# Retention's gated result: from a DRAM round trip to parts formed out of the transposes' PSUM banks, with the head's pieces moved by a step

## Chip, cores and metric

One NeuronCore of a Trainium2 chip runs the whole program. The metric is device time in microseconds (us) of one execution: the median of three timed runs, with lowest and highest. Beside them stands one execution under the hardware profiler, from which all rows of the trace come.

## The reference

A decoder trunk of two layers on 512 tokens of width 2048, in float32. Layer 0 is multi-scale retention, layer 1 latent attention; the change lies in layer 0 and at its output projection.

```python
proj = h @ w_in
q, k, v, g = jnp.split(proj, [RET_QK, 2 * RET_QK, 2 * RET_QK + RET_WIDTH], axis=-1)
q = rope(q.reshape(B, S, RET_HEADS, RET_DK), pos)              # 8 heads of 256
k = rope(k.reshape(B, S, RET_HEADS, RET_DK), pos) * (RET_DK ** -0.5)
v = v.reshape(B, S, RET_HEADS, RET_DV)                         # 8 heads of 512
y = chunkwise_retention(q, k, v)
mu = jnp.mean(y, axis=-1, keepdims=True)
var = jnp.mean(jnp.square(y - mu), axis=-1, keepdims=True)
y = (y - mu) * lax.rsqrt(var + EPS)
y = (y.reshape(B, S, RET_WIDTH) * gn_g.astype(jnp.float32)).astype(h.dtype)
return (jax.nn.silu(g) * y) @ w_out                            # 4096 -> 2048
```

Around it stand RMSNorm with a modulated shift and scale (`ada_w`, computed from the conditioning vector), a modulated gate and a residual add.

## The kernel before

**Exact parts.** Every product of two float32 matrices runs as three TensorE (PE) matmuls on two parts: `hi` is the value rounded to the matmul's format and `lo` the rest, and hi\*hi, hi\*lo and lo\*hi are summed in PSUM (`mm3`, L157). The helper `split` (L132) makes them: ScalarE (ACT) copies the source into `hi` (L133) and VectorE (DVE) subtracts (L134).

**Steps.** The middle of the program is a list of steps. One step holds the weights of one unit (load by SP, `split` on ACT and DVE), its matmuls, what follows them (copies out of PSUM), and `beside`: extra loads, forms and matmuls of other work. For step i the driver (L1290 on) issues, in this order: weight loads for up to three steps ahead, the step's extra loads, the split of the weights of step i+1, the extra forms, the step's matmuls, its extra matmuls, the additions of a "modulation row" that was loaded at the end of the step before, the load of the next row, and the copies that follow. `behind` keeps each engine's queue in that order; a small amount of reordering is left to the scheduler. Weights of a step are 128 x 2 x 512; raw, high and low tiles have three buffers each. A modulation row (L820, L829) is a 512 KB load and one DVE operation, later summed on PE by matmuls with one output column (`sum_modulation`, L842), in steps marked `banks_free`.

**Blocks.** I call sixteen steps a block. Block p is the query/key projection of heads 6 and 7. Blocks n = 0 to 3 are the output projection, contraction rows of heads 2n and 2n+1: in each block four rounds r (512 output columns) of four units u, 24 matmuls of 512 columns a step. A unit u reads the input parts `o1_in[n, u]` (two row blocks of 128 features); units 0 and 1 come from the even head, 2 and 3 from the odd one. Running sums stay in four `acc` banks in a round; at its end ACT keeps them in SBUF (L1060) and from n=1 on seeds the next round from there (L1057).

**A head beside the steps.** `retention(h)` (L887) returns a list of pieces, one for each step. Heads 0 and 1 run beside block p, 2 and 3 beside block 0, and so on; the even head's piece k stands in step k, the odd head's in step k+4. Before the change there are 13 pieces:

| piece | load | form (ACT, DVE) | matmuls |
|---|---|---|---|
| 0 | `load_qk(0)` | | |
| 1, 2 | `load_qk(1)` in 2 | rotary, query halves | |
| 4, 5 | `load_decay` in 5 | rotary, key halves | |
| 7 | | | `scores`, into four `aux` banks |
| 8 | `load_v` | `decay_scores` (L932) | |
| 9 | `load_gates` | `split_v` | `values`, into four `aux` banks |
| 10 | | `group_norm` (L959 to L971) | |
| 11 | | `gate` (L977) | `transposes` (L984), into four `aux` banks |
| 12 | | `store` (L992, L994) and DMA on POOL's queue (L996) | |

Queries, keys, values and gates wait in DRAM from the projection. There are four `aux` banks, so each use has to wait until the banks of the one before are read. For head 0, silu of the gate multiplies after the transposes (L994), for the others before (L977).

**The way to the projection.** `store` multiplies the transposed result by the norm's gain and POOL writes it to `y2_d`, four blocks of 128 rows a head. `o1_input` (L1080) loads two such blocks at a time on SP's queue into one tile with a single buffer (L1087) and splits it with L133 and L134. These loads and splits stand in the last two steps of a block and the first three of the next, beside the weights of those steps. In the profile the tiles are called `y` or `y_d`, `o_in`, `o_h` and `o_l`, and the projection's weights `o_r`, `o_whi`, `o_wlo`.

**Shared buffers that the change touches.** `tmp`: six tiles of 128 x 512. `big`: sixteen tiles for parts; they hold the layer's input until block p has read it, then rotary queries and keys, values, and the projection's input parts. `yn`: four tiles, for raw values as well as normalised rows, and for copies of head 7's queries and keys on their way to DRAM.

## Time and profile before

| | us |
|---|---|
| median of three runs (lowest, highest) | 2272.65 (2268.16, 2273.11) |
| the profiled execution | 2269.27 |
| its span, first to last instruction | 2267.5 |
| TensorE busy in the span | 2195.1 |
| VectorE busy | 1522.6 |
| ScalarE busy | 992.5 |
| mean granted TensorE clock | 0.99 |

Times in the trace count from the span's start. Block p runs from about 943 to 1060, the blocks 0 to 3 from 1060 to about 1510. A row of a group reads: line, engine, operation, output<-inputs, sizes and count, then busy time in us, mean ns of one, and idle time of the engine before them with what ended it. A row of waits reads: who waited for whom, total us, times, the longest. Neighbouring instructions of one engine overlap a little at their ends in these records, so that a row of several can be shorter than their sum.

### The profile page before, as it was taken

The page shows a single profiled execution, that of the slowest core. Times are in us where ns is not written, and L with a number is a line of the kernel's source. Part 1 is how long each engine was busy: PE and PEld are TensorE (multiplying, and loading weights), DVE is VectorE, ACT ScalarE, POOL GpSimd, SP SyncE. Part 2 cuts the span into 40 slices and gives each one's busy share as a digit, 9 for nine tenths or more (in the row PEclk, how much of TensorE's full clock was granted, in tenths as well). Part 3 has the DMA queues.
Part 4 walks back from the last instruction along what each step waited for, and adds up shares of the span by engine and source line. Part 5 has one row for each costly group of instructions (what it writes and reads, how often), then busy time and mean ns, then how long its engine had stood idle before and what let it go on. Part 6 is the DMA issues. An engine that isn't in the chain of part 4 may idle for free.

```text
span 2267.5 us, 27960 instructions
## 1 busy us (share of the span) xinstructions
PE 2195.1 (97%) x10198; PEld 1820.5 (80%) x10198; DVE 1522.6 (67%) x2242; ACT 992.5 (44%) x1486; POOL 131.7 (6%) x237
## 2 busy tenths in 40 slices
PE   5999999999999999999999999999999999999997
PEld 4887888888888888887887878777888888888886
DVE  7997867676667788665867676455454367777545
ACT  5664434334343444433344444445322255555433
POOL 1000000100000000001010100110000000000000
PEclk8999999999999999999999999999999999999999
DMA  9975685867676777746656474742466432225433
GB/s 343 351 230 168 200 298 178 282 196 262 222 242 235 229 249 267 246 150 220 224 196 232 176 252 149 239 150 80 130 222 217 158 108 79 91 98 172 149 126 116
DMA packets 243563, 449.73 MB, mean 198 GB/s; under 512 B 22024, under 2 KB 95840, under 8 KB 243424
## 3 DMA queue, kind: packets, MB, share of 16 engines
q1 hardware_dynamic: 228016, 400.88, 54.0%
q0 software_dynamic: 14976, 46.78, 5.2%
q8 instruction: 80, 1.31, 0.2%
q14 instruction: 59, 0.48, 0.1%
q10 hardware_dynamic: 432, 0.27, 0.0%
HBM read 396.98 MB, written 50.87 MB: 198 GB/s over the span
## 4 chain that ended last, share of the span: by engine, by line
PE 69%; issue 13%; DVE 7%; DMA 5%; ACT 4%; POOL 1%; SPq 0%; POOLq 0%; DVEq 0%; ACTq 0%
PE o L1116 6%; PE qk L161 4%; PE qk L159 4%; PE qk L160 4%; PE g L161 3%; PE g L159 3%; PE g L160 3%; PE o L160 2%; PE o L159 2%; PE o L161 2%; DMA aw<-in_ada_w_dram 2%; PE x L695 2%; PE y L696 2%; PE x L696 2%; PE y L695 2%
## 5 line engine op out<-in xcount | busy, mean ns | idle before, releaser
L1116 PE MATMUL o<-o_whi,o_h 128*128 128x512 f32 x496 | 196.0, 395 | 12.4 <-ACT o_h L133 12.0
L1116 PE MATMUL o<-o_whi,o_l 128*128 128x512 f32 x496 | 194.0, 393 | 2.0 <-DVE o_l L134 2.0
L1116 PE MATMUL o<-o_wlo,o_h 128*128 128x512 f32 x496 | 194.4, 392 | 0.0
L159 PE MATMUL qk<-hT,qk_h 128*128 128x512 f32 x448 | 176.2, 393 | 0.0
L161 PE MATMUL qk<-hT,qk_l 128*128 128x512 f32 x448 | 175.4, 391 | 0.0
L160 PE MATMUL qk<-hT,qk_h 128*128 128x512 f32 x448 | 175.2, 391 | 0.0
L829 DVE SCALAR_TENSOR_TENSOR mod_am<-mod_aw,cact,mod_am 128x1024 f32<-128x1024 f32 x120 | 153.5, 1279 | 10.3 <-DMA mod_aw<-in_ada_w_dram 10.0
L134 DVE TENSOR_TENSOR o_wlo<-o_r,o_whi 128x1024 fp32r<-128x1024 f32 x62 | 75.7, 1223 | 75.5 <-ACT o_whi L133 75.4
L1116 PEld LDWEIGHTS o<-o_whi,o_h 128*128 128x128 f32 x496 | 94.0, 189 | 33.6 <-ACT o_h L133 14.2
L1116 PEld LDWEIGHTS o<-o_whi,o_l 128*128 128x128 f32 x496 | 93.8, 189 | 24.1 <-DVE o_l L134 4.5
L134 DVE TENSOR_TENSOR o_l<-o_in,o_h 128x1024 fp32r<-128x1024 f32 x40 | 49.0, 1224 | 90.3 <-ACT o_h L133 90.2
L1116 PEld LDWEIGHTS o<-o_wlo,o_h 128*128 128x128 f32 x496 | 93.9, 189 | 19.1
L134 DVE TENSOR_TENSOR qk_l<-qk_r,qk_h 128x1024 fp32r<-128x1024 f32 x56 | 68.1, 1223 | 60.4 <-ACT qk_h L133 58.9
L159 PE MATMUL g<-h,g_hi 128*128 128x512 f32 x256 | 100.7, 393 | 1.1 <-ACT ckv_n L1451 1.1
L159 PE MATMUL o<-o_w_hi,o_h 128*128 128x512 f32 x256 | 100.1, 391 | 0.0
L160 PE MATMUL o<-o_w_lo,o_h 128*128 128x512 f32 x256 | 99.9, 390 | 0.0
L161 PE MATMUL g<-h,g_lo 128*128 128x512 f32 x256 | 99.7, 390 | 0.0
L160 PE MATMUL g<-h,g_hi 128*128 128x512 f32 x256 | 99.7, 390 | 0.0
L161 PE MATMUL o<-o_w_hi,o_l 128*128 128x512 f32 x256 | 99.6, 390 | 0.0
L161 PEld LDWEIGHTS qk<-hT,qk_l 128*128 128x128 f32 x448 | 84.5, 189 | 18.6 <-DVE qk_l L134 1.1
L160 PEld LDWEIGHTS qk<-hT,qk_h 128*128 128x128 f32 x448 | 84.5, 189 | 18.0 <-issue 0.5
L159 PEld LDWEIGHTS qk<-hT,qk_h 128*128 128x128 f32 x448 | 84.5, 189 | 17.8 <-ACT qk_h L133 0.2
(1355 smaller groups left out, 5790.3 us busy)
## 6 DMA issues: line engine op xcount, KB each, us to landing
mod_aw<-in_ada_w_dram SPq DMA_DIRECT2D x128, 512.0 KB, 5.1
aw<-in_ada_w_dram SPq DMA_DIRECT2D x128, 256.0 KB, 6.1
o_r<-in_ret_w_out_dram SPq DMA_DIRECT2D x64, 512.0 KB, 5.4
qk_r<-in_ret_w_in_dram SPq DMA_DIRECT2D x112, 256.0 KB, 3.4
g_raw<-in_mla_w_in_dram SPq DMA_DIRECT2D x32, 512.0 KB, 3.6
o_w_raw<-in_mla_w_out_dram SPq DMA_DIRECT2D x32, 512.0 KB, 3.7
qk_d<-qk_st POOLq DMA_DIRECT2D x32, 256.0 KB, 3.9
qk_r<-qk_d SPq DMA_DIRECT2D x32, 256.0 KB, 6.2
```

What stands on the lines that cost most here:

```text
L134: DVE.tensor_sub(lo, src, hi.bitcast(F32))
L159: PE.matmul(o, lhs[0], rhs[0], start=first and not seeded, stop=False, skip_group_check=seeded)
L160: PE.matmul(o, lhs[0], rhs[1], start=False, stop=False, skip_group_check=seeded)
L161: return PE.matmul(o, lhs[1], rhs[0], start=False, stop=last, skip_group_check=seeded)
L695: PE.matmul(banks[b], a[0], w[1], start=False, stop=False, skip_group_check=True)
L696: PE.matmul(banks[b], a[1], w[0], start=False, stop=True, skip_group_check=True)
L829: DVE.scalar_tensor_tensor(out=am, in0=aw, scalar=ck, in1=am, op0=ALU.mult, op1=ALU.add)
L1116: PE.matmul(o, a[i], w[j][:, ki, cols], start=first and i + j == 0, stop=last and i == 1, skip_group_check=True)
```

## The change

The DRAM tensor `y2_d`, the stores to it, `o1_input` and its 16 loads and splits are taken out. In place of `store`, `form_input` writes the two parts straight from the transposes' banks: ACT scales the bank into `hi`; the full value goes to a `tmp` tile, by ACT for the odd row blocks and by DVE for the even ones; DVE subtracts. For head 0 DVE makes the gated value and ACT copies it to `hi`. Only `big` tiles are written, in the order in which the units read them.

The list has 14 pieces now: `load_qk(1)` in 3 in place of 2, `scores` in 6 in place of 7, `load_decay` in 7 in place of 5, `transposes` in 12 in place of 11, the last form in 13 in place of 12. Values are loaded to a tag of their own, `vr`, with four buffers. Modulation rows stand in other steps of a block, still 11 of 16, and `banks_free` is set in two steps in place of four. Head 7's queries and keys leave through `tmp`.

```diff
-                fetch(f"v{t}", "yn", v_d, h * T + t * P)
+                fetch(f"v{t}", "vr", v_d, h * T + t * P)
...
-        def store():
+        def form_input():
+
             for j, ps in enumerate(aside["yT"]):
-                y2 = l1_tile("y2", 2, f"y2_{h}_{j}") if j % 2 else tmp(f"y2_{h}_{j}")
+                if j % 2 == 0:
+                    hi, lo = (big(f"o1_{p}{h}_{j}") for p in "hl")
+                    o1_in[h // 2, h % 2 * 2 + j // 2] = hi, lo
                 gn = gn_c[:, h * 4 + j : h * 4 + j + 1]
-                if h > 0:
-                    ACT.activation(y2, ps, AF.Identity, scale=gn)
+                hj, lj = hi[:, j % 2, :], lo[:, j % 2, :]
+                f = tmp(f"y2_{h}_{j}")
+                if h == 0:
+                    DVE.scalar_tensor_tensor(out=f, in0=ps, scalar=gn, in1=sg[j], op0=ALU.mult, op1=ALU.mult)
+                    ACT.copy(hj, f)
                 else:
-                    DVE.scalar_tensor_tensor(out=y2, in0=ps, scalar=gn, in1=sg[j], op0=ALU.mult, op1=ALU.mult)
-                r0 = (h * 4 + j) * P
-                POOL.dma_start(y2_d[r0 : r0 + P, :], y2)
+                    ACT.activation(hj, ps, AF.Identity, scale=gn)
+                    if j % 2:
+                        ACT.activation(f, ps, AF.Identity, scale=gn)
+                    else:
+                        DVE.tensor_scalar(out=f, in0=ps, scalar1=gn, scalar2=None, op0=ALU.mult)
+                DVE.tensor_sub(lj, f, hj.bitcast(F32))
 
         return [
             {"load": lambda: load_qk(0)},
             {"form": lambda: rope(0, 0)},
-            {"load": lambda: load_qk(1), "form": lambda: rope(0, 1)},
-            {},
+            {"form": lambda: rope(0, 1)},
+            {"load": lambda: load_qk(1)},
             {"form": lambda: rope(1, 0)},
-            {"load": load_decay, "form": lambda: rope(1, 1)},
-            {},
+            {"form": lambda: rope(1, 1)},
             {"multiply": scores},
+            {"load": load_decay},
             {"load": load_v, "form": decay_scores},
             {"load": load_gates, "form": split_v, "multiply": values},
             {"form": group_norm},
-            {"form": gate, "multiply": transposes},
-            {"form": store},
+            {"form": gate},
+            {"multiply": transposes},
+            {"form": form_input},
         ]
...
-        for i in range(4):
+        for i in (2, 3):
             block[i].banks_free = True
...
-                own=tmp if h == 6 else lambda name: l1_tile("yn", 4, name),
+                own=tmp,
...
-        light(block, (0, 1, 2, 3, 4, 6, 7, 11, 12, 13, 15))
+        light(block, (0, 2, 3, 4, 6, 7, 10, 11, 12, 14, 15))
...
-    for n in range(4):
-        for u in range(4):
-            load, prepare = o1_input(n, u)
-            i = n_p + 16 * (n + 1) + u
-            if u < 2:
-                steps[i - 2].beside["load"].append(load)
-                steps[i].units.append((None, prepare))
-            else:
-                steps[i - 1].beside["load"].append(load)
-                steps[i - 1].beside["form"].append(prepare)
```

More of the change, by code (lines that the diff above doesn't have):

```diff
@@ L86, in hybrid_trunk_kernel @@
     g_d = dram.tile([RH * T, T], F32, name="g_d")
-    y2_d = dram.tile([RH * T, T], F32, name="y2_d")
     x1_d = dram.tile([T, D], F32, name="x1_d")
@@ L876, in hybrid_trunk_kernel @@
     n_odd = [0]
-    rotary = []
+    rotary, o1_in = [], {}
     def rope_half(b1, b2, second, dst, name):
@@ L1060, in keep_sums @@
         ACT.copy(x1_block(t, r), o1_banks[n, r, t])
-    o1_res, o1_gates, o1_in = {}, {}, {}
+    o1_res, o1_gates = {}, {}
     def load_residual(r, t, tag):
@@ L1078, in x1_out @@
         POOL.dma_start(x1_d[t * P : (t + 1) * P, r * T : (r + 1) * T], v)
-    def o1_input(n, u):
-        raw = []
-        r0 = (4 * n + u) * 2 * P
-        def load():
-            raw.append(l1_tile("in", 1, f"o1_in{n}_{u}", (P, 2, T)))
-            nc.sync.dma_start(raw[0], y2_d[r0 : r0 + 2 * P, :].rearrange("(k p) n -> p k n", p=P))
-        def prepare():
-            o1_in[n, u] = big(f"o1_h{n}_{u}"), big(f"o1_l{n}_{u}")
-            split(raw[0], *o1_in[n, u])
-        return load, prepare
     def o1_unit(n, r, u, kn, cn, where=(("whi", 3), ("wlo", 3))):
@@ L1200, in hybrid_trunk_kernel @@
         block[5].beside["form"].append(lambda t=t: seed(3, 0, t))
-        block[0].beside["load"].append(lambda t=t: load_residual(3, t, "yn"))
+        block[0].beside["load"].append(lambda t=t: load_residual(3, t, "vr"))
         block[2].beside["load"].append(lambda t=t: load_residual(2, t, "ld"))
-        block[5].beside["load"].append(lambda t=t: load_residual(0, t, "yn"))
+        block[5].beside["load"].append(lambda t=t: load_residual(0, t, "vr"))
         block[9].beside["load"].append(lambda t=t: load_residual(1, t, "ld"))
@@ L1270, in hybrid_trunk_kernel @@
     later = all_rows()
-    loads = [load for step in steps for load, _ in step.units if load is not None]
+    loads = [load for step in steps for load, _ in step.units]
     fetched = []
@@ L1278, in prepare_for @@
                 prepare()
-        return sum(load is not None for load, _ in units)
+        return len(units)
     with behind(S_):
```

## The prediction, on record before the changed kernel ran

> **What bounds the kernel now.** I read the page's first part, then busy time by stretch, then TensorE's waits in the part that the change touches, then the chain of waits, then the granted clock.

> ```profile
> span 2267.5 us, 27960 instructions
> PE 2195.1 (97%) x10198; PEld 1820.5 (80%) x10198; DVE 1522.6 (67%) x2242; ACT 992.5 (44%) x1486; POOL 131.7 (6%) x237
> ```

> TensorE (PE) is busy for 97% of the span: the change can win only what PE idles, or runs slowly, where retention meets the output projection. Its blocks by stretch (us, then busy time and instructions of PE, its weight loads, DVE, ACT and POOL, then granted clock, DMA share, GB/s):

> ```profile
> 1060.00:1184.00 124.00, 118.05 (x542) 97.81 (x541) 84.51 (x120) 55.49 (x83) 10.04 (x17) 0.99 0.62 220
> 1184.00:1305.00 121.00, 114.59 (x532) 94.87 (x531) 81.44 (x118) 56.36 (x85) 7.56 (x12) 0.99 0.62 214
> 1305.00:1425.00 120.00, 116.80 (x541) 96.44 (x540) 79.19 (x118) 55.76 (x84) 6.52 (x10) 1.00 0.60 204
> ```

> PE idles 5.95, 6.41 and 3.20 us in them; DVE is free for 39 us or more in each. What PE waits for between 946 and 1510 us (total, times, longest):

> ```profile
> PE o L1116 <- ACT o_h L133: 12.0, 4, 5.0
> PE s L159 <- ACT y L992: 2.7, 3, 1.1
> PE o L1116 <- DVE o_l L134: 2.0, 4, 0.5
> PE mod_ps L842 <- ACT y L992: 1.3, 1, 1.3
> PE yT L984 <- DVE yn L977: 0.4, 2, 0.2
> ```

> 18.4 us. The first and third are the projection's input parts; the second and fourth are PE wanting an `aux` bank that `store` has not read yet; the fifth is `gate` and `transposes` in one step. The chain shows what the first consists of (start, duration):

> ```profile
> 1183.45 6.11 DMA y_d<-y
> 1189.68 4.11 DMA o_in<-y_d
> 1193.81 1.05 ACT o_h L133
> 1194.88 1.24 DVE o_l L134
> ```

> From the write's start to the last part 12.7 us pass, more than two 5.45 us steps (a row below). The longest of these waits cost more than their length. Two stretches behind a wait, and one at full clock:

> ```profile
> 1076.50:1079.90 3.40, 3.21 (x8) 2.53 (x9) 3.23 (x3) 1.09 (x2) 0.00 (x0) 0.51 0.90 323
> ...
> 1196.00:1199.40 3.40, 3.24 (x8) 2.56 (x9) 3.40 (x5) 0.00 (x0) 0.00 (x0) 0.50 0.82 284
> 1199.40:1202.80 3.40, 3.40 (x16) 2.78 (x15) 1.91 (x4) 1.99 (x3) 0.00 (x0) 1.00 0.79 284
> ```

> After two of the four waits (5.0 us the longest) the clock is granted at half: 8 matmuls fall into 3.4 us in place of 15 (at 0.227 us, from 48 in 10.90 us below), so 7 x 0.227 = 1.6 us are lost each, 3.2 us together.

> **The change part by part.** The durations:

> ```profile
> L134 DVE TENSOR_TENSOR o_l<-o_in,o_h 128x1024 fp32r<-128x1024 f32 x16 | 19.6, 1224 | 33.9 <-ACT o_h L133 33.8
> ...
> L992 ACT ACTIVATE y<-yT,vcol 128x512 f32<-128x512 f32 x28 | 16.9, 692 | 0.0
> ...
> L133 ACT CAST o_h<-o_in 128x1024 fp32r<-128x1024 f32 x16 | 16.9, 1054 | 44.0 <-DMA o_in<-y_d 44.0
> ```

> ```profile
> L1467 ACT ACTIVATE cqT<-cqT,vcol 128x512 fp32r<-128x512 f32 x4 | 2.4, 691 | 0.0
> ...
> L1469 DVE TENSOR_SCALAR cqT_3f<-cqT,vcol 128x512 f32<-128x512 f32 x1 | 0.7, 744 | 0.0
> ```

> *The round trip.* Removed: 32 stores on POOL's queue, 16 loads on SP's, 16 casts on ACT (16.9 us) and 16 subtractions on DVE (19.6). Added, for each of heads 1 to 7: six ACT passes from the bank (0.691 each, the form that the low-rank path already runs) in place of four, two DVE passes (0.744) and four 512-wide subtractions (0.62 each, from the row of four below). So ACT pays 4 x 1.054 less and 4 x 0.691 more in a block, -1.5 us; DVE pays 4 x 1.224 less and 2 x (2 x 0.744 + 4 x 0.62) more, +3.0 us. On averages that is hidden: 81.44 + 3.0 of some 115 us. Head 0 forms with four scaled products on DVE and four casts on ACT, in a block without modulation rows.

> An even head now has parts 0 and 1 formed in step 13 for step 16, three steps ahead; an odd one has parts 2 and 3 formed in step 1 for steps 2 and 3. There the transposes end step 0, the first pair needs 3 x 0.691 = 2.1 us of ACT and one subtraction, 2.7 us, against a step of 5.45. So lines one and three of PE's waits go: 14.0 us, and 3.2 us of half clock. What would be late next at that place is the weights' low part, which DVE has made a step before, ahead of the form in its queue.

> *The pieces moved.* `transposes` one step after `gate`: 0.4 us. Odd-head scores now stand in step 10, even transposes in step 12, no longer in one step, so the 2.7 us go. The four `aux` banks then pass scores(6), values(9), odd scores(10), transposes(12), odd values(13), odd transposes(0 of the next block). Each hand-over is a possible new wait. I take them in turn, from block n=1 (PE and chain first, then ACT, then DVE):

> ```profile
> 1251.88 10.90 PE o L1116 x48
> ```

> ```profile
> 1262.60 1.91 PE L984 MATMUL yT<-ident,yn 128*128 128x128 f32 x16
> ```

> ```profile
> 1254.65 2.79 ACT L971 ACTIVATE yn<-y,nmr,gn_r 128x512 f32<-128x512 f32 x4 [6.34 <-DVE nmr L965]
> ...
> 1263.42 0.59 ACT L1057 COPY o<-x 128x512 f32<-128x512 f32 x1
> 1263.94 1.04 ACT L133 CAST o_whi<-o_r 128x1024 fp32r<-128x1024 f32 x1
> ```

> ```profile
> 1234.29 0.68 DVE L932 TENSOR_TENSOR s_0f<-s,dec 128x512 f32<-128x512 f32 x1
> ...
> 1237.89 0.28 DVE L134 TENSOR_TENSOR sT<-s_3f,sT 128x128 fp32r<-128x128 f32 x1
> ...
> 1242.28 2.49 DVE L134 TENSOR_TENSOR v<-v_r,v 128x512 fp32r<-128x512 f32 x4
> ...
> 1261.95 1.28 DVE L829 SCALAR_TENSOR_TENSOR mod_am<-mod_aw,cact,mod_am 128x1024 f32<-128x1024 f32 x1
> 1265.02 1.23 DVE L134 TENSOR_TENSOR o_wlo<-o_r,o_whi 128x1024 fp32r<-128x1024 f32 x1 [1.78 <-ACT o_whi L133]
> ```

> Two steps are 10.90 us, so a step 5.45. Values end at 1251.88 and the first normalised row ends at 1254.65 + 0.70, 3.5 us on: odd scores after step 10 find their first bank free 2 us early, and no wait is charged.

> Odd values in step 13 are the tight one. Let T be the end of step 11's products (1262.60 here). Behind the kept sums the next weights' cast and subtraction end at 1266.25, T+3.65. Then DVE has the decay group, 3.9 us with a 0.7 us rotary operation inside, so 3.2 (T+6.9), a modulation row 1.2 (T+8.1), the weights for step 14 1.15 (T+9.2), the new form of the even head 2 x 0.66 + 4 x 0.62 = 3.8 (T+13.0), and only then the first value part, T+13.7. PE ends step 12 and the transposes at T+7.4, step 13 at T+12.85, and the build's order puts four products ahead that need high parts alone, 0.9 us: T+13.7. It meets exactly. Without the overlap of about 0.08 us that the group of four shows (2.49 us for four), the twelve instructions come 1 us later, and ACT's cast of the first value part could come 0.4 us late: 1.5 us. With a row fewer it is nothing. I take 0.5 us, in blocks 0 to 2: +1.5 us, bounds 0 and 4.5. Queued behind the form on DVE are the value parts, then step 15's weights, which have the 7 us of values as cover. If the form found no cover, its 3.8 us would stand on PE's path eight times, 30 us.

> Even transposes in step 12 want the last score bank at T + 5.45 + 3/4 x 1.91 = T+6.9, and DVE ends the group with that bank at T+6.9: 0, at most 0.3 x 3.

> Two modulation sums of one-column products: the one that waited 1.3 us behind the transposes at block n=2's step 0 moves to step 2, where banks are free. But the last one now stands in block n=3's step 1 directly behind head 7's transposes, with all banks held until the form's first two reads, 0.7 us and a hand-over. I charge +1.3, the same wait in the new place, bounds 0.8 and 1.5; its cover would be a free bank. What such products can do to the clock, after a row of the chain with 32 of them:

> ```profile
> 942.69 3.47 PE mod_ps L842 x32
> ```

> ```profile
> 946.80:950.20 3.40, 3.40 (x10) 2.65 (x8) 1.87 (x4) 0.28 (x1) 0.00 (x0) 0.50 0.89 258
> 1298.10:1303.70 5.60, 4.12 (x34) 3.60 (x33) 5.43 (x6) 3.64 (x6) 1.68 (x3) 1.00 0.97 341
> ```

> Behind the 32, at 946.80, the clock is halved. The second stretch is transposes, a 1.3 us wait and 16 one-column products, as the new place will be, and its clock stayed at 1.00: I charge nothing, with 1.6 us as the upper bound. [...]

> *Loads moved.* The second query/key load stands one step before its rotary piece instead of two, the decay one before its use instead of three; value loads leave the tag of `yn`. Their time to land, and SP's waits now:

> ```profile
> qk_r<-qk_d SPq DMA_DIRECT2D x32, 256.0 KB, 6.2
> ...
> dec<-const_decay_dram SPq DMA_DIRECT2D x8, 256.0 KB, 4.0
> ```

> ```profile
> SPq L1087 <- DVE o_l L134: 68.1, 8, 16.2
> ...
> SPq L1087 <- DMA y_d<-y: 31.5, 5, 8.1
> ```

> 6.2 against a step of 5.45 looks late, but SP runs a step ahead of DVE's forms (it issues when a raw weight buffer is free), and loses the two blocking waits shown: 0 charged, bounds 0 and 0.7 x 8 on DVE, off PE's path.

> Sum: -14.0 - 3.2 - 2.7 - 1.3 - 0.4 + 1.5 + 1.3 = -18.8 us. The profiled execution took 2269.27 us (span 2267.5 plus 1.8 around it), so 2250.5. The runs shown have a median 3.4 us higher, 2272.65. I set the sum against the mean of the four executions, 2270.8: **2252 us**. Own range: -21.6 with every new wait at nothing from 2268.2, 2246.6; all at their upper bounds (4.5 + 0.9 + 1.5, and 1.6 of clock), -13.1, from 2273.1, 2260.

> **The rivals.**
> *Half is given back.* Idle time goes from the inputs to other parts that are late: DVE does more in step 13 and step 1 and weights' low parts take over. For it: DVE's 3.0 us more and the exact meeting above. Against: DVE still has some 30 us idle in a block (115 less 84.4). Price: half of 18.8, 2261.

> *No change.* The result's parts come early but PE then meets a limit that ran along, weight DMA say. For it: 0.62 DMA share and 220 GB/s. Against: the change takes 16 MB of traffic away, and no weight wait stands among PE's. Price: 2271.

> *Slower.* DVE stands in order; a query/key load issued a step later and landing after its turn holds DVE, and with it the weights' subtraction behind it. Against it: DVE's lead over PE. It decides if SP issues only as the step begins and DVE has no lead: then 6.2 less the 1.2 us of weights in front, 5.0 us, for each of 8 heads is 40, less the 21.6 saved, +18: 2289. To be slower at all needs 2.7 us lost per head.

> **How the numbers follow.** Forecast 0.74, half 0.12, no change 0.07, slower 0.07. The range must reach the second case and leave out the last two: 2246 to 2265. A measurement of this kernel tells 0.2% (4.5 us) from no change; both first cases lie beyond it: faster 0.86, same 0.07, slower 0.07.

> **What would show it.** In PE's waits no `o_h` or `o_l` wait remains in the four blocks, nor `s <- y`; a `mod_ps` wait of about 1.3 us stands once; `y` waits for `v` by 0 to 1.5 us in three blocks; the half-clock stretches in blocks 0 and 1 are gone; the stretch 1060 to 1510 is about 19 us shorter, everything before 940 as it was. Wrong if PE waits for `o_wlo`, if DVE idles on `qk_r` or `dec` for several us in each block, or if odd values wait over 2 us.

## The result, and the profile after

| | before | after |
|---|---|---|
| median of six runs each (lowest, highest), us | 2271.01 (2268.16, 2273.11) | 2255.78 (2253.38, 2257.62) |
| the profiled execution, us | 2269.27 | 2255.62 |
| ratio after/before, 95% interval | | 0.9934 (0.9921 to 0.9947) |

The change makes the kernel 15.2 us faster. The forecast was 2252 in a range of 2246 to 2265, so direction and range hold. The median is 3.8 us above the forecast, and the experiments below show that one step left out of the sum cost more than that. The page of the kernel after, its first lines:

```profile
span 2253.9 us, 27801 instructions
PE 2193.4 (97%) x10198; PEld 1819.2 (81%) x10198; DVE 1528.9 (68%) x2272; ACT 988.6 (44%) x1488; POOL 113.8 (5%) x205
```

TensorE does the same 10198 matmuls; POOL lost the 32 stores. Where the time went shows in the stretches block p, blocks 0 to 3, and the rest, cut at the same instructions in both traces: the last product ahead of block p, the first product of the output projection, the first transpose of its result. The columns are as in the prediction. Before:

```profile
942.30:1060.50 118.20, 117.66 (x558) 98.73 (x556) 67.89 (x109) 38.86 (x57) 9.11 (x15) 0.99 0.54 181
1060.50:1511.40 450.90, 432.39 (x1980) 357.23 (x1981) 286.41 (x409) 201.70 (x308) 32.91 (x54) 0.99 0.61 212
1511.40:2267.40 756.00, 728.55 (x3621) 611.45 (x3619) 446.25 (x826) 323.07 (x573) 31.53 (x56) 0.99 0.41 133
```

After:

```profile
943.80:1065.80 122.00, 117.83 (x542) 97.80 (x541) 68.44 (x112) 41.28 (x61) 8.21 (x14) 0.97 0.50 164
1065.80:1498.30 432.50, 430.51 (x1997) 357.74 (x1996) 292.37 (x436) 195.13 (x305) 15.82 (x24) 1.00 0.56 185
1498.30:2253.80 755.50, 728.62 (x3622) 611.12 (x3619) 446.16 (x826) 323.06 (x573) 31.52 (x56) 0.99 0.42 134
```

The blocks of the output projection are 18.4 us shorter. The rest is the same within 0.5. But block p, for which the forecast's sum has no term, is 3.8 us longer, although it has 16 matmuls fewer: the transposes of head 1 (1.9 us) now stand in block 0. Ahead of block p the profiled execution of after is 1.5 us later, in code that the change does not touch. So 1.5 + 3.8 - 18.4 - 0.5 = -13.6, the difference of the two spans. TensorE's waits in the kernel after, from 930 to 1500 us:

```profile
PE qk L158 <- ACT qk_h L132: 3.4, 1, 3.4
PE y L159 <- DVE v L133: 1.0, 3, 0.4
PE s L158 <- ACT yn L970: 0.9, 4, 0.3
PE qk L160 <- DVE qk_l L133: 0.5, 1, 0.5
PE mod_ps L841 <- DVE y L1003: 0.3, 1, 0.3
```

All five lines that the prediction showed are gone, and a sixth that it did not list (0.4 us for `qk_st`). In their place stands a wait that it did not have: the query/key projection itself waits for its weights' parts in block p, 3.4 + 0.5 us.

**What holds the weights.** The query/key weights pass through ACT and DVE in order, behind the rotary pieces of head 0. DVE, ACT and TensorE there, in the kernel after (start, duration, idle time before):

```profile
965.41 0.69 DVE L881 TENSOR_TENSOR rope_t<-qk_r,cos 128x512 f32<-128x512 f32 x1 [15.38 <-DMA qk_r<-qk_d]
...
967.56 0.62 ACT L132 CAST qk_0p<-rope_t 128x512 fp32r<-128x512 f32 x1 [18.96 <-DVE rope_t L883]
968.08 1.04 ACT L132 CAST qk_h<-qk_r 128x1024 fp32r<-128x1024 f32 x1
...
969.17 0.50 PE L158 MATMUL qk<-hT,qk_h 128*128 128x512 f32 x1 [3.39 <-ACT qk_h L132]
```

DVE stood 15.38 us for head 0's loaded queries. ACT, in order, stood 18.96 us in front of the cast that needs DVE, and the next weights' cast was queued behind that one. The load was late because SP issued it late. SP's first load of block p, before and then after:

```profile
946.23 0.34 SPq L1299 DMA_DIRECT2D cos<-tables_d  x1
```

```profile
958.62 0.34 SPq L1283 DMA_DIRECT2D cos<-tables_d  x1
```

And SP's waits between 930 and 965, before and then after:

```profile
SPq L1299 <- PE mod_ps L842: 2.5, 1, 2.5
```

```profile
SPq L1283 <- PE mod_ps L841: 12.6, 1, 12.6
```

SP waits for the one-column products of the modulation sums. Where block p begins, the pool `lp` ends and `l1` opens in its memory; the wait says that `cos` and its neighbours lie where the summed modulation rows lay, so no load of block p starts before `sum_modulation` has read them. The change moved that sum: `banks_free` now holds in steps 2 and 3, not 0 to 3, and block p uses the same function `light` as the other blocks.

**The clock.** Two stretches at half clock in the kernel after (the others of before at 1076 and 1196 are gone):

```profile
969.90:973.30 3.40, 2.88 (x8) 2.29 (x8) 2.68 (x5) 0.96 (x2) 0.00 (x0) 0.50 0.54 154
1417.00:1420.40 3.40, 3.40 (x10) 2.62 (x10) 2.69 (x6) 1.06 (x2) 0.00 (x0) 0.51 0.02 5
```

The first follows the 3.4 us wait. The second follows the place that the prediction named, in block 3:

```profile
1412.91 1.91 PE L983 MATMUL yT<-ident,yn 128*128 128x128 f32 x16
1415.08 1.95 PE L841 MATMUL mod_ps<-ones,mod_am 128*128 128x1 f32 x16 [0.26 <-DVE y L1003]
```

With the one behind block p's 32 one-column products, the stretches at half clock from block p to block 3 start at 959.68, 969.92 and 1417.06 in this execution: 10.24 and 447.14 us apart, 3 and 131 times 3.413, the length that the trace lists for one of them. The expectations below call such steps the clock's windows.

### The profile page after: what moved, and what is told of

Same layout as the page of the kernel before. It is cut to its first block, busy times and chain, and to the rows that moved or that the text cites. A ratio compares the mean times of both kernels' runs of the same rounds, so it can differ in the third digit from the quotient of the medians.

```text
span 2253.9 us, 27801 instructions
## 1 busy us (share of the span) xinstructions
PE 2193.4 (97%) x10198; PEld 1819.2 (81%) x10198; DVE 1528.9 (68%) x2272; ACT 988.6 (44%) x1488; POOL 113.8 (5%) x205
## 4 chain that ended last, share of the span: by engine, by line
PE 76%; issue 10%; DVE 7%; ACT 5%; DMA 1%; POOL 0%; SPq 0%; POOLq 0%; DVEq 0%; ACTq 0%
PE o L1110 12%; PE qk L160 4%; PE qk L159 4%; PE qk L158 4%; PE g L158 3%; PE g L159 3%; PE g L160 3%; PE o L158 2%; PE o L160 2%; PE o L159 2%; PE x L694 2%; PE y L695 2%; PE x L695 2%; PE y L693 2%; PE y L694 2%
## 5 line engine op out<-in xcount | busy, mean ns | idle before, releaser
L159 PE MATMUL qk<-hT,qk_h 128*128 128x512 f32 x448 | 175.4, 392 | 0.0
L133 DVE TENSOR_TENSOR o_wlo<-o_r,o_whi 128x1024 fp32r<-128x1024 f32 x62 | 75.7, 1223 | 87.8 <-ACT o_whi L132 87.7
L1110 PEld LDWEIGHTS o<-o_whi,o_l 128*128 128x128 f32 x496 | 93.5, 189 | 19.6
L133 DVE TENSOR_TENSOR qk_l<-qk_r,qk_h 128x1024 fp32r<-128x1024 f32 x56 | 68.1, 1222 | 60.2 <-ACT qk_h L132 59.7
L159 PE MATMUL o<-o_w_lo,o_h 128*128 128x512 f32 x256 | 99.8, 390 | 0.0
L159 PE MATMUL g<-h,g_hi 128*128 128x512 f32 x256 | 99.6, 389 | 0.0
L159 PEld LDWEIGHTS qk<-hT,qk_h 128*128 128x128 f32 x448 | 84.8, 189 | 18.1 <-issue 0.5
L132 ACT CAST qk_h<-qk_r 128x1024 fp32r<-128x1024 f32 x56 | 57.9, 1049 | 88.5 <-PE qk L159 63.5
## 6 DMA issues: line engine op xcount, KB each, us to landing
aw<-in_ada_w_dram SPq DMA_DIRECT2D x128, 256.0 KB, 6.0
qk_r<-in_ret_w_in_dram SPq DMA_DIRECT2D x112, 256.0 KB, 3.9
qk_d<-qk_st POOLq DMA_DIRECT2D x32, 256.0 KB, 3.9
qk_r<-qk_d SPq DMA_DIRECT2D x32, 256.0 KB, 6.2
```

Of the source, the lines that this page charges most:

```text
L132: ACT.copy(hi, src)
L133: DVE.tensor_sub(lo, src, hi.bitcast(F32))
L159: PE.matmul(o, lhs[0], rhs[1], start=False, stop=False, skip_group_check=seeded)
L1110: PE.matmul(o, a[i], w[j][:, ki, cols], start=first and i + j == 0, stop=last and i == 1, skip_group_check=True)
```

## The experiments

Eight kernels ran, in two groups of four, each beside runs of the kernel before on the same chip. The kernel after ran in neither group; its own ratio is 0.9934 (0.9921 to 0.9947). The intervals of e1, e8 and e9 lie below that one. Those of e3, e4 and e7 overlap it, and for these the traces carry the argument.

| kernel | median us | before beside it | ratio, 95% |
|---|---|---|---|
| e1, sums of block p first | 2250.0 | 2271.84 | 0.9904 (0.9891 to 0.9918) |
| e2, kernel before, sums late | 2279.03 | 2271.84 | 1.0035 (1.0024 to 1.0047) |
| e3, last sum apart | 2253.33 | 2271.84 | 0.9918 (0.9904 to 0.9931) |
| e4, old places, no round trip | 2251.52 | 2271.84 | 0.9911 (0.9898 to 0.9925) |
| e5, kernel before, pieces moved | 2273.81 | 2270.35 | 1.0015 (1.0006 to 1.0024) |
| e7, filler in the wait | 2253.4 | 2270.35 | 0.9928 (0.9915 to 0.994) |
| e8, both repairs, sums split | 2246.84 | 2270.35 | 0.9895 (0.9882 to 0.9909) |
| e9, both repairs | 2249.14 | 2270.35 | 0.9902 (0.9888 to 0.9915) |

**e1: the sums of block p ahead of its step 0 again.**

```diff
     light(block, ())
+    block[0].banks_free = True
```

> The kernel after, with the modulation sums of block p ahead of its step 0 again (as before the change) instead of step 2; all else of the change stays. Theory H (held loads): in the kernel after, the first loads of block p (cos, L1283) lie in addresses that the modulation's rows held, so SP waits 12.6 us for the moved sums, the query and key loads come late, the vector engine idles 15.4 us, and TensorE waits 3.4 + 0.5 us at 965.8 and 969.9 and runs a 3.4 us stretch at half clock. Then here SP's first load goes about 12 us earlier, the waits for qk_h and qk_l are gone and the half-clock stretch at 969.9 too: 3.9 + 1.6 = 5.5 us less than the kernel after, about 2250.3 against 2255.8 (2248.5 to 2252). Rival L (late by the new places of load_qk(1) and load_decay) and rival T (the staging tiles of head 7, now in tmp, crowd it): the waits stay, 2255.8 within 1.5.

Measured 2250.0, in the middle of what theory H said. SP's wait is back to its old size, SP's first load goes at 947.15, and TensorE's waits from 930 to 1490 have no `qk` line. SP's wait, then TensorE's three:

```profile
SPq L1284 <- PE mod_ps L841: 2.4, 1, 2.4
```

```profile
PE y L159 <- DVE v L133: 1.0, 3, 0.4
PE s L158 <- ACT yn L970: 1.0, 4, 0.3
PE mod_ps L841 <- DVE y L1003: 0.3, 1, 0.3
```

The stretches of e1, block p and blocks 0 to 3:

```profile
943.20:1057.70 114.50, 114.22 (x542) 95.79 (x541) 68.57 (x112) 41.48 (x61) 8.22 (x14) 1.00 0.54 175
1057.70:1490.30 432.60, 430.55 (x1997) 357.81 (x1996) 292.50 (x436) 195.17 (x305) 15.82 (x24) 1.00 0.56 185
```

Block p falls from 122.0 to 114.5 and the blocks behind it stay (432.5, 432.6). `load_qk(1)` and `load_decay` are still at their new places and head 7's tiles still in `tmp`, so rivals L and T fall. Of the 7.5 us in this pair of profiled executions, 3.9 are the waits and 1.6 the half clock at 969.9; most of the remaining 2 us is a half-clock stretch that follows the 32 one-column products in the profiled executions of before (946.8) and after (959.7) and not in this one (clock 1.00 over block p). The medians, 5.8 us apart, are nearer to the 5.5 expected.

**e2: the kernel before, with the sums of block p late.**

```diff
     light(block, ())
+    block[0].banks_free = block[1].banks_free = False
```

> The kernel before, with the modulation sums of block p at step 2 instead of step 0 and nothing else changed. Theory H: SP's first load of block p waits some 12 us for the sums, the vector engine idles about 15 us, TensorE waits about 4 us in steps 2 to 4 of block p and may lose a half-clock stretch (1.6): 2275 to 2277 against 2271. Rivals L and T: no wait comes, 2271 within 1.5.

Measured 2279.03: 7.2 us slower than before, theory H's direction and 2 to 4 us above its range. One line of TensorE's waits, one of SP's, and the clock behind the wait:

```profile
PE qk L159 <- ACT qk_h L133: 3.6, 1, 3.6
```

```profile
SPq L1300 <- PE mod_ps L842: 12.3, 1, 12.3
```

```profile
967.10:973.90 6.80, 6.35 (x14) 4.57 (x15) 5.57 (x10) 2.87 (x4) 0.00 (x0) 0.50 0.66 199
```

The same wait appears in a kernel that has nothing else of the change, which shows that the moved sums alone cause it. Here the half clock lasted 6.8 us, two of the usual stretches. The extra over what was expected goes with half clock: three more stretches of 6.8 us and one of 3.4 stand in blocks 0 to 3 of this execution, where the kernel before has two of 3.4.

**e3: the last sum behind its step's products.**

```diff
-    block[1].banks_free = True
+    block[1].beside["multiply"].append(sum_modulation)
```

> The kernel after, with the last modulation sum (16 one-column products, block 3 step 1) behind that step's 24 products instead of ahead of them, so that it no longer follows the 16 transposes of step 0. Theory C (the clock falls because transposes, a short wait and one-column products lie in one row, some 4 us with little for TensorE): no half-clock stretch between 1400 and 1500, TensorE's waits as in the kernel after less the 0.3 for y: 1.6 to 1.9 less, about 2254.0 (2253 to 2255). Rival D (the stretch is only where the clock's windows happen to end): a stretch stays somewhere in block 3, 2255.8 within 1.

Measured 2253.33, 2.4 us under the kernel after by medians whose spreads overlap; the trace is clearer. The four blocks, and the place of the old half-clock stretch:

```profile
1069.00:1499.50 430.50, 428.71 (x1998) 356.63 (x1997) 292.49 (x436) 195.17 (x305) 15.87 (x24) 1.00 0.56 186
1409.00:1425.00 16.00, 16.00 (x89) 13.75 (x87) 8.58 (x11) 6.62 (x9) 0.00 (x0) 1.00 0.61 197
```

The blocks lose 2.0 us (432.5 to 430.5): the 0.26 us wait and the half-clock stretch. The same 16 transposes and 16 one-column products still run within these 16 us, with 24 full products between them, and the clock stays at 1.00. e9 and e8, which carry the same edit, also keep 1.00 over the four blocks (430.5 us each). Theory C holds, rival D has nothing left in block 3.

**e4: the input formed from the banks, at the pieces' old places.** (With e1's line as well.)

```diff
-            {"form": lambda: rope(0, 1)},
-            {"load": lambda: load_qk(1)},
+            {"load": lambda: load_qk(1), "form": lambda: rope(0, 1)},
+            {},
             {"form": lambda: rope(1, 0)},
-            {"form": lambda: rope(1, 1)},
+            {"load": load_decay, "form": lambda: rope(1, 1)},
+            {},
             {"multiply": scores},
-            {"load": load_decay},
...
-            {"form": gate},
-            {"multiply": transposes},
+            {"form": gate, "multiply": transposes},
```

> The output projection's input formed from the banks as in the kernel after, but the head's pieces at the places they had before (scores in piece 7, transposes with the gate in piece 11, input formed in piece 12; load_qk(1) and load_decay where they were), and the sums of block p ahead of step 0 as before. Theory R (the way through DRAM alone cost the waits for o_h and o_l): they are gone, 14.0 less, and with them the half-clock stretches at 1076 and 1196, 3.2 less; the waits of scores for y (2.7), of mod_ps (1.3) and of yT (0.4) stay: 2271.0 - 17.2 = 2253.8 (2252 to 2256). Rival M (the moved pieces are what takes the waits away, since the scores then run earlier and the vector engine gets to the input in time): over half of the waits for o_h and o_l stay, 2261 to 2268.

Measured 2251.52, a little under theory R's range. TensorE's two lines of waits from 930 to 1494, and the four blocks:

```profile
PE s L158 <- ACT y L1001: 6.2, 3, 2.3
PE s L158 <- DVE y L996: 0.2, 1, 0.2
```

```profile
1061.70:1494.70 433.00, 426.85 (x1983) 357.27 (x1982) 294.74 (x436) 192.73 (x304) 15.02 (x23) 1.00 0.56 183
```

No wait for `o_h` or `o_l` is left: the way through DRAM was the cause, and rival M falls. (e4 keeps the rest of the change, the modulation rows' new steps and the tag `vr`; these were not tried alone.) Theory R had three waits wrong. The scores' did not stay at 2.7 but grew to 6.2; the likely reason is that the form reads the transposes' banks twice, on ACT and DVE, where `store` read them once, and the odd head's scores want those banks in the same step. The waits of `mod_ps` (1.3) and `yT` (0.4) did not stay. So by the rows of waits the moved pieces pay for what the form adds. That they make the kernel faster is not shown: e4 lies 1.5 us above e1 with overlapping intervals.

**e5: pieces moved in the kernel before, even heads only.**

```diff
+        if h % 2 == 0:
+            pieces[6:8] = pieces[7], pieces[6]
+            pieces[11:13] = {"form": gate}, {"multiply": transposes}, {"form": store}
+        return pieces
```

> The kernel before with its way through DRAM, where only the even heads take the new places of the moved pieces (scores in piece 6, transposes in piece 12, store in piece 13); the odd heads stay, since their input would otherwise be loaded before it is stored. The scores of the odd head now stand behind transposes instead of running beside them: theory S says that the 2.7 us of scores waiting for y go for the even-odd pairs and nothing else changes, with the odd heads' store as late as before: o_h and o_l still 14.0, both half-clock stretches still there, 2268 to 2270 against 2271.8. Rival: the even store a step later makes its loads late too, o_h waits 2 to 4 us more, 2272 to 2275.

Measured 2273.81, 3.5 us slower, in the rival's range but not for the rival's reason. TensorE's first lines of waits:

```profile
PE o L1120 <- ACT o_h L133: 12.6, 4, 5.2
PE yT L984 <- DVE yn L977: 3.5, 12, 0.7
```

The scores' 2.7 us are gone, as theory S said, and `o_h` grew by 0.6 only. But transposes now wait twelve times for gated rows, 3.5 us where it was 0.4, and both expectations missed that. It is not what made the kernel slower: within blocks 0 to 3 the waits come to 18.6 us, as before. The four blocks, and the first of their stretches at half clock:

```profile
1060.70:1516.50 455.80, 437.44 (x1980) 359.76 (x1981) 283.94 (x409) 202.38 (x309) 32.90 (x54) 0.98 0.61 209
1075.90:1082.70 6.80, 5.47 (x13) 4.31 (x14) 5.45 (x6) 1.99 (x2) 0.00 (x0) 0.51 0.94 313
```

The blocks are 4.9 us longer than before (450.9), and TensorE is busy 5.0 us longer for the same 1980 matmuls. The half clock lasted 6.8, 6.8 and 3.4 us (from 1075.9, 1195.4 and 1441.1), where the kernel before has 3.4 twice: three more stretches of 3.4 us, 4.8 us at 1.6 each. Without the new form the moved pieces gain nothing.

**e7: eight unused products in the wait.**

```diff
+    def filler():
+        ps = aux("filler")
+        for _ in range(8):
+            PE.matmul(ps, hT[0][:, 0, 0:P], hT[0][:, 0, :], start=True, stop=True)
+
+    block[2].beside["multiply"].append(filler)
```

> The kernel after with 8 unused full products (128x512, 0.228 us apart by its trace, 1.8 us) put behind step 2 of block p, where TensorE waits 3.4 us for qk_h in step 3. Nothing of the computation is left out. Theory C (the half-clock stretch at 969.9 is the answer to a 3.4 us window that was nearly all idle): the wait shrinks to about 1.6 us, the products cost nothing of their own, and the half-clock stretch behind it is gone: 1.7 less than the kernel after, 2254.1 (2253 to 2255.5). Rival D (the clock answers to the wait itself, or to the 32 one-column products before it): the half-clock stretch stays, 2255.8 (2255 to 2258).

Measured 2253.4, 2.4 us less than the kernel after for 8 products more, by medians whose spreads overlap. TensorE there, then the clock:

```profile
965.48 1.98 PE L1051 MATMUL filler<-hT 128*128 128x512 f32 x8
969.26 0.50 PE L158 MATMUL qk<-hT,qk_h 128*128 128x512 f32 x1 [1.81 <-ACT qk_h L132]
```

```profile
968.60:972.00 3.40, 2.74 (x12) 2.28 (x13) 3.11 (x5) 0.61 (x1) 0.00 (x0) 1.00 0.33 85
972.00:975.40 3.40, 3.40 (x17) 2.79 (x16) 2.45 (x6) 2.52 (x3) 0.00 (x0) 1.00 0.81 255
```

The wait ends at the same point of the program, only filled. Behind it, after a pause of 1.81 us, the clock stays at 1.00, where the kernel after, with a pause of 3.39, ran 8 products in 3.4 us. e2 and e3, which wait 3.6 and 3.8 us there without a filler, also have half clock behind it. So the half clock at 969.9 answers to the empty time, not to the late weights and not to the one-column products 11 us earlier (which have their own stretch, in both kernels).

**e9 and e8: the two repairs together, and with the sums of block p in two steps.** e9 is e1 and e3. e8 adds:

```diff
-    def sum_modulation(age=2):
+    def sum_modulation(age=2, most=9):
-        while ripe and clock[0] - ripe[0][0] >= age:
+        while ripe and clock[0] - ripe[0][0] >= age and most:
+            most -= 1
...
+    block[0].banks_free = block[1].banks_free = True
...
-                sum_modulation()
+                sum_modulation(most=1 if i < n_p + 2 else 9)
```

> Both repairs together: the sums of block p ahead of step 0 as in e1, the last sum behind the products of block 3 step 1 as in e3. If the two losses are separate, as theories H and C say, their gains add: 5.5 and 1.7 to 1.9 less than the kernel after, 2248.4 (2247 to 2250), no wait of TensorE over 0.5 us and no half-clock stretch between 1060 and 1490. Rival: the clock's windows take another place and a half-clock stretch comes back elsewhere: 2250.

> As e9, but with the two sums of block p in two steps (16 one-column products ahead of step 0, 16 ahead of step 1), so that no 3.4 us of one-column products lie in one row. Theory C: no half-clock stretch between 940 and 1490 in any phase of the clock's windows, at most 1.7 less than e9: 2246.7 to 2248.4. Rival H2 (SP's first load waits for the later of the two sums, a step longer): the loads of block p go some 6 us later than in e1, and TensorE waits 0 to 2 us in step 3: 2248 to 2251.

e9 measured 2249.14 and e8 2246.84, both faster than the kernel after. The repairs of e1 and e3 take effect where they should; block p and the four blocks of e9:

```profile
943.50:1058.00 114.50, 114.24 (x542) 95.80 (x542) 68.44 (x112) 41.37 (x61) 8.22 (x14) 1.00 0.54 175
1058.00:1488.50 430.50, 428.70 (x1997) 356.61 (x1997) 292.48 (x436) 195.15 (x305) 15.83 (x24) 1.00 0.56 186
```

These are e1's block p and e3's four blocks, so the two losses are separate. Whether splitting the sums helps further is not settled. In e8 SP does wait longer, as rival H2 said (7.8 us, where e1 has 2.4), but TensorE waits only 0.4 us for it; its block p took 115.3 us, no less than e9's 114.5, and the intervals of the two ratios overlap. What splitting could save is a half-clock stretch behind the 32 products, and e9's profiled execution had none there. The 32 stand in one row in nine of the ten profiled executions; half clock follows in six (before, after, e2, e3, e4, e7) and not in three (e1, e5, e9).

## Why the prediction was right, and where it was not

**The round trip, -14.0.** Right: no `o_h` or `o_l` wait remains, in the kernel after or in e4, which has the form without the moved pieces.

**The half clock, -3.2.** The two stretches are gone. One came back in block 3, where the sum charged nothing and gave 1.6 as the upper bound. To charge nothing because the second row's clock had stayed at 1.00 was the wrong choice: that row was one execution. The same row, transposes, a 1.3 us wait and 16 one-column products, kept the clock at 1.00 in e5 too, but in e2 the clock fell during its products:

```profile
1310.63 2.46 PE L842 MATMUL mod_ps<-ones,mod_am 128*128 128x1 f32 x16 [1.30 <-ACT y L992]
```

```profile
1311.90:1318.70 6.80, 6.80 (x21) 5.54 (x21) 4.50 (x8) 1.96 (x3) 1.19 (x3) 0.50 0.95 367
```

In the new place the transposes, 0.26 us of waiting and 16 one-column products are 4 us with no full product, and the clock halved behind them in all three profiled executions that have them in this order (the kernel after, e1 at 1409.3, e7 at 1415.8). The old row was hit in e2 and missed in the kernel before and e5; what decides that was not shown.

**Scores and transposes, -2.7, -1.3, -0.4.** Right in size: all three waits are gone. For the first two the given reason holds, with one addition that e4 shows: without the move the scores' wait is 6.2, so by the rows of waits the move was worth more inside this change than the 2.7 read off the trace of before. The 0.4 also went in e4, where transposes stand in `gate`'s step, so the move is not what takes it away. "No wait is charged" for the odd scores behind the normalised rows was 0.9 us too low (4 waits of 0.2 to 0.3, three of them in blocks 0 to 2).

**Odd values, +1.5.** Three waits of 0.4 at most, 1.0 in all, inside the bounds of 0 and 4.5.

**The last sum, +1.3.** The wait was 0.3, below the lower bound of 0.8. The prediction counted the reads from the end of all transposes, but the bank that the sum wants is the first of four, full three quarters of 1.91 = 1.4 us earlier, and its reads run beside the other transposes (ACT's first starts at 1413.55 and DVE's at 1414.27, the transposes run from 1412.91 to 1414.82). The real price of this place was the clock.

**What failed: the sum has no term between 940 and 1060.** In "Two modulation sums of one-column products" the prediction costed those at blocks n=2 and n=3, and passed over the two of block p, which the same line of `light` moves from step 0 to step 2. It asked what waits for the banks of a moved sum, and not what waits for the rows that the sum reads. That is SP, at the exchange of one pool for the next, and all loads of block p behind it. Price: 3.9 us of waits and 1.6 of half clock in the trace, 5.8 by the medians of the kernel after and e1. With that step undone the median is 2250.0, 2 us below the forecast of 2252. So the 3.8 us by which the forecast missed are this loss less some 2 us that the rest of the program gave beyond the sum; that the two partly cancel is luck. The mechanism is the one of the rival "slower" (DVE held in order by a late load, weights behind it), in one place instead of eight, and from a cause that the rival did not name: its own cause, the loads moved by a step, cost nothing (e1). The prediction's sign for it, DVE idle on `qk_r`, came once.

**The sum for blocks 0 to 3.** Waits there fell from 18.6 us to 1.9, half clock from 3.2 to 1.6, and head 1's transposes came in with 1.9: -16.7 - 1.6 + 1.9 = -16.4. Measured -18.4. About 1.1 us more comes from the pipeline by the estimate below; some 0.9 stay unexplained.

## What to carry to other kernels

When an edit delays a reader, ask what its source buffer becomes next, not only what its output feeds: here the memory of a pool that closes went to the next pool's first loads, and one late reader held SP for 12.6 us in place of 2.5, and with it loads that nobody had moved. A flag shared by all blocks (`banks_free`) has to be costed in every block that uses it. And keep full-width products between transposes and one-column products: here the clock halved behind such a row of 4.0 us in all three profiled executions that have it in block 3, as it did behind a pause, although TensorE was busy for 3.75 us of it (the kernel after); with 24 full products in between it stayed at 1.00 (e3).

## What the runs showed of the hardware

**A wait cost more than its row.** Full products start 0.23 us apart here but each is listed with 0.39 (the profile models the ends), so they overlap in the listing. Two neighbours around the longest wait of the kernel before:

```profile
1071.32 0.39 PE L1116 MATMUL o<-o_whi,o_l 128*128 128x512 f32 x1
1076.69 0.80 PE L1116 MATMUL o<-o_whi,o_h 128*128 128x512 f32 x1 [4.98 <-ACT o_h L133]
```

From start to start are 5.37 us; less the usual 0.23, the wait of 4.98 cost 5.14, 0.16 more. By the rows of waits blocks 0 to 3 had 14 of them before and have 7 now. If each costs the same 0.16, an estimate from this one wait, that is 7 x 0.16 = 1.1 us of gain that those rows do not show.

**Of two pauses of like length, one had half clock behind it.** In e4 the scores paused 2.27 us behind transposes, and the clock fell to 0.51; in the kernel before a pause of 2.37 us (one of its four waits for `o_h`) left it at 1.00. e4, TensorE and then the clock:

```profile
1251.47 1.91 PE L983 MATMUL yT<-ident,yn 128*128 128x128 f32 x16
1255.65 0.50 PE L158 MATMUL s<-qk_0p,qk_0p 128*128 128x512 f32 x1 [2.27 <-ACT y L1001]
```

```profile
1256.10:1259.50 3.40, 3.40 (x11) 2.90 (x10) 2.81 (x6) 1.78 (x4) 0.00 (x0) 0.51 0.76 290
```

The kernel before, in and behind the pause of 2.37 us:

```profile
1432.70:1436.10 3.40, 1.03 (x4) 0.30 (x2) 0.65 (x1) 1.73 (x2) 0.00 (x0) 1.00 0.95 308
1436.10:1439.50 3.40, 2.87 (x13) 2.31 (x13) 1.95 (x4) 0.26 (x1) 0.00 (x0) 1.00 1.04 386
```
